# Which tiles the opening group of matmuls holds: five gate tiles in place of one branch's values and the second queries

## The chip, the cores and the metric

The kernel runs on one core of a Trainium2 chip. The metric is the device time of one execution in microseconds, the median of several runs. A profile of one execution (its page and its trace) is at hand beside the times.

## What is computed

One decoder layer on x (1 x 512 x 1024) with a condition vector c. Everything is float32. Cut to what matters here:

```python
mod = c @ w_ada + b_ada                       # six vectors of 1024: shift, scale and gate for both sub-layers
u = x * (1.0 + sc1) + sh1
proj = u @ w_in                               # q,k,v of branch A (fox), forget logits, q,k,v of branch B (stick-breaking), two gates
y_fox = softmax(q k^T/8 + c_t - c_s, causal) @ v      # 8 heads of 64, c the running sum of log sigmoid of the forget logits
y_sb  = A @ v,  A[t,s] = beta[t,s] * prod_{s<j<t} (1 - beta[t,j]),  beta = sigmoid(q k^T/8)   # 8 heads, s < t
merged = sigmoid(g_a) * (y_fox @ w_fox_proj) + sigmoid(g_b) * (y_sb @ w_sb_proj)
x = layer_norm(ALPHA * x + (1.0 + gt1) * (merged @ w_o))
h = causal_depthwise_conv((x * (1.0 + sc2) + sh2) @ w_up)
x = layer_norm(ALPHA * x + (1.0 + gt2) * ((silu(h_gate) * h_val) @ w_down))
```

## The kernel before

Every large product is made of three matmuls. An operand is split into a high part, which ACT rounds (`hi_of`, L76), and a low part, which DVE subtracts (`lo_of`, L79); high times high, high times low and low times high are summed in PSUM (L117 to L119 in `mm3`). In the code branch 1 is stick-breaking and branch 0 is fox. `PAIRS` puts the four pairs of stick-breaking heads ahead of the four fox pairs. Where a row of the profile says uh and ul, these are the two parts of u, kept for the whole attention part.

**The opening.** Eight PSUM banks `grp[0..7]` are accumulated over eight rounds j (L258 to L296), one for each 128 rows of w_in. A round loads two tiles of w_ada, 904 columns of w_in (`W1C`) and a block of x; DVE sums the condition's products (L171), ACT forms u, and PE runs 23 matmuls (L274): three for each of the banks 0 to 6 and two for bank 7. Bank 0 holds the queries of pair 0, bank 1 its keys, bank 2 the queries of pair 1, banks 3 to 6 the values of branch 1 in four blocks of tokens, bank 7 the forget logits. In the last round the banks are finished one after the other, in the order 0, 1, 2, 7, 3 to 6.

**The stream of filler.** Everything else that is projected from u is written into a list, `stream`, whose entries are generators that yield after three matmuls: `proj` (a tile of w_in of 128 columns, 24 matmuls into a new bank, then what is done with it), `vproj` (a block of values, 24 matmuls, L415 to L417), `bproj` (the projection of a branch's output, the merge), `ada_split` and `ada_sum` (the gate vector of the condition). `fill(n)` runs n matmuls of the list and `fill_to(mark)` runs up to a mark. `lim` holds a mark which `fill` doesn't pass: `y1` until head 7 has its output, then `y0`, then the end. The list's entries take weights from `items`, in order: `weights(i, ahead)` issues loads on SP's queue into four staging slots (`raw`, L133) up to item i + 3, and lets ACT and DVE process the items (split them, or sum them) up to item i + `ahead`, or earlier when a slot must be had. Among the items stand tiles of w_ada (`add_ada`, `ada_proc`): sums on DVE along the row (L171) or by column (L551). `skip` says how many of the first places for them are left out; all 24 that belong here are in the list by the end of the merge. The weights of branch 0's values are four items (`add_wv`), split into sixteen tiles of 128 x 512 (`v_proc`), and `vproj` uses them ahead of pair 4's queries.

**The attention.** The order of the heads' stages is written out at the end of the part. A head has `stage_a` (scores, L439 and L440, a mask for fox at L445, then for stick-breaking two sigmoids on ACT, a scan on DVE at L478 and a product on POOL at L479, for fox a maximum at L461, exponentials at L462 and a scaling at L467), `stage_b` (ten transposes on PE, L499, and their split) and `stage_c` (eight matmuls with the values, L517, then ytmp at L523 on ACT, yf at L524 on DVE, and on each second head yh on ACT and yl on DVE). Two heads ahead runs stage a, one ahead stage b, with fill between (`FILL`). `q_evac` and `k_evac` bring queries and keys into their parts s and m (DVE at L366 and L79); `v_evac` brings values into vv; `gate_after` takes a sigmoid of a gate's bank into sg (L580). Ahead of the first head stand the evacuations of the opening's banks with some fill between them. Most SBUF tiles of this part come from one pool of 60 (`NZ`), and PSUM is a pool of eight banks: a new tile waits for the last reader of the one that had its place.

Of the kernel before, what the change touches and what calls it, by code (L numbers as in the profile page):

```python
# [16 lines left out]
P = 128  # L17
T = 512
D = 1024
KT = D // P  # L20
NB = T // P
# [4 lines left out]
EPS = 1e-5  # L26
NEG = -1.0e30
W1C = 904
VC = slice(384, 896)
PAIRS = [(1, p) for p in range(4)] + [(0, p) for p in range(4)]  # L30
TILES = [("k", 1)]
TILES += [(c, p) for p in range(2, 8) for c in "qk"]
TILES += [("sb", j) for j in range(KT)] + [("fox", j) for j in range(KT)]
NZ = 60
LOADS = 4
WBUFS = 3
# [10 lines left out]
def layer_kernel(ctx: ExitStack, tc: tile.TileContext, out, xT, x, cT, crow, wa0, wa1, bcol, bgt, w1, wct, wv, bf,  # L47
# [74 lines left out]
    items = []  # L122
    state = {"load": 0, "proc": 0}

    def add_item(src, proc, cols=1024):
        items.append([src, proc, cols, None, None])
        return len(items) - 1

    def weights(i, ahead=AHEAD):
        while state["load"] < min(len(items), i + LOADS):  # L130
            it = items[state["load"]]
            it[3] = stg.tile([P, 1024], F32, name=nm("raw"), tag="raw", bufs=LOADS)
            nc.sync.dma_start(it[3][:, 0 : it[2]], it[0])  # L133
            state["load"] += 1
            while state["proc"] <= state["load"] - LOADS:
                process()
        while state["proc"] < min(len(items), i + 1 + ahead):
            process()
        return items[i][4]
# [19 lines left out]
    grp = [bank() for _ in range(8)]  # L159
# [98 lines left out]
    def first_ops(j, g):  # L258
        h, l = pend[j][2:4]
        a, b = uh[j], ul[j]  # L260
        if g == 7:
            return [(fpad[:, j, :], a), (fpad[:, j, :], b)]
        if g < 3:
            c = slice(g * P, (g + 1) * P)
            return [(h[:, c], a), (l[:, c], a), (h[:, c], b)]
        c = slice((g - 3) * P, (g - 2) * P)
        return [(a[:, c], h[:, VC]), (a[:, c], l[:, VC]), (b[:, c], h[:, VC])]

    def first_mm(j, gs):
        ops = [(g, n, m) for g in gs for n, m in enumerate(first_ops(j, g))]  # L270
        if j < KT - 1:
            ops.sort(key=lambda o: o[1] + 3 * (o[0] == 7))
        for g, n, (w, u) in ops:
            PE.matmul(grp[g], w, u, start=j == 0 and n == 0, stop=j == KT - 1 and n == (1 if g == 7 else 2))  # L274
# [6 lines left out]
    for j in range(KT):  # L281
        if j + 2 < KT:
            first_load(j + 2)
        if j + 1 < KT:
            with tc.issue_after(state["u"].ins):
                first_split(j + 1)
            with tc.issue_after(state["after"].ins):
                first_acc(j + 1)
        if j < KT - 1:
            first_mm(j, range(5))  # L290
        if j + 1 < KT:
            first_mod(j + 1)
        if j < KT - 1:
            first_mm(j, range(5, 8))
        else:
            first_mm(j, (0, 1, 2, 7, 3, 4, 5, 6))  # L296

    st0.close()

# [98 lines left out]
        return vt[(br, j, h // 4)][:, o : o + P]  # L398

    def v_proc(r):  # L400
        for e in range(2):
            h, l = z(F32R, "wvh"), z(F32R, "wvl")
            hi_of(h, r[:, e * 512 : (e + 1) * 512])
            lo_of(l, r[:, e * 512 : (e + 1) * 512], h)
            wvs.append((h, l))

    wvs = []

    def vproj(j, last):
        ps = bank()  # L410
        weights(last, 0)
        tb = slice(j * P, (j + 1) * P)
        for k in range(KT):
            h, l = wvs[k]
            PE.matmul(ps, uh[k][:, tb], h, start=k == 0, stop=False)  # L415
            PE.matmul(ps, uh[k][:, tb], l, start=False, stop=False)
            PE.matmul(ps, ul[k][:, tb], h, start=False, stop=k == KT - 1)  # L417
            yield 3
        for half in range(2):
            v_evac(0, j, half, ps)  # L420

    def proj(n, after):
        ps = bank()
# [198 lines left out]
    stream, sums = [], []  # L622
    adas = [0]

    skip = [15]

    def add_ada(n=1):
        for _ in range(n):
# [9 lines left out]
    marks = {}  # L638
# [17 lines left out]
    def add_pair(p):  # L656
        br, pr = seq[p]
        for c, ev in (("q", q_evac), ("k", k_evac)):
            if (c, p) in TILES:
                add_proj((c, p), lambda ps, ev=ev: ev(br, pr, ps))  # L660
                marks[(p, c)] = len(stream)
                add_ada(1 + (p > 4))
                add_wv(p)

    wvi = []

    def add_wv(p):
        if p >= 3 and len(wvi) < 4:
            wvi.append(add_item(wv[len(wvi)], v_proc))

    def add_gate(br, j):
        add_proj(("sb" if br == 1 else "fox", j), gate_after(br, j))
        add_ada(1 + (br == 0))

    gb = list(range(KT))
    for p, ng in ((1, 1), (2, 2), (3, 2), (4, 3)):
        if p == 4:
            for j in range(NB):
                stream.append((vproj, (j, wvi[-1])))
        add_pair(p)  # L680
        for _ in range(ng):
            add_gate(1, gb.pop(0))
            add_wv(p)
    marks["y1"] = len(stream)
    bj = list(range(KT))
    for p in (5, 6, 7):
        add_pair(p)
        for _ in range(3):
            if bj:
                j = bj.pop(0)  # L690
# [56 lines left out]
            fill(3)  # L747

    lim[0] = marks["y1"]
    q_evac(1, 0, grp[0])  # L750
    k_evac(1, 0, grp[1])
    forget_evac()
    q_evac(1, 1, grp[2])
    fill(6)
    stage_a(1, 0)
    for half in range(2):
        for j in range(NB):
            v_evac(1, j, half, grp[3 + j])
        fill(6)
    stage_a(1, 1)  # L760
    fill(12)
    stage_b(1, 0)
    heads = [(br, 2 * p + e) for br, p in seq for e in range(2)]
    last = hd[heads[1]]['last']
    for n, (b, h) in enumerate(heads):
        if n == 4:
            forget(last)
        f1, f2, f3 = FILL[n // 8]
        if n + 2 < 16:
            if n % 2 == 0:  # L770
                fill_to(marks[(n // 2 + 1, "k")])
            last = hd[heads[n + 1]].get("last")
            stage_a(*heads[n + 2])
        fill(f1)
        if n + 1 < 16:
            stage_b(*heads[n + 1])
        fill(f2)
        stage_c(b, h)
        if n == 7:
            lim[0] = marks["y0"]  # L780
        if n == 15:
            lim[0] = len(stream)
        fill(f3)
# [133 lines left out]
    for n in range(2 * FT):  # L917
        if n < NSPLIT:
            h, l = items[wui[n]][4]
            ps = bks[n]  # L920
# [84 lines left out]
def _pack(inputs):  # L1005
    import numpy as np

    a = {k: np.ascontiguousarray(v) for k, v in inputs.items()}
    c = np.ascontiguousarray
    w_in, w_ada = a["w_in"], a["w_ada"]  # L1010
    wk = w_ada.reshape(KT, P, 6, D)
    r = {}
    r["xT"] = c(a["x"][0].T)
    r["x"] = a["x"][0]
    r["cT"] = c(a["c"][0].reshape(KT, P).T)
    r["crow"] = a["c"]
    wt = c(w_ada.T).reshape(6, KT, P, D)
    r["wa0"] = c(wt[0:2].transpose(1, 0, 2, 3))
    kf = wk[:, :, [2, 5]].reshape(4, 2, P, 2, 2, 512).transpose(3, 4, 0, 2, 1, 5).reshape(2, 8, P, D)
    r["wa1"] = c(np.concatenate([kf[0], wt[3], wt[4], kf[1]], axis=0))  # L1020
    bm = a["b_ada"].reshape(6, KT, P)
    r["bcol"] = c(bm[[0, 1, 3, 4]].transpose(2, 0, 1))
    r["bgt"] = c(a["b_ada"].reshape(6, D)[[2, 5]])
    def col(kind, n):
        if kind in ("sb", "fox"):
            return (4104 if kind == "sb" else 3080) + n * P
        br, p = PAIRS[n]
        return 1544 * br + 512 * "qkv".index(kind) + p * P

    first = [w_in[:, s : s + P] for s in (col("q", 0), col("k", 0), col("q", 1))]  # L1030
    cols = np.concatenate(first + [w_in[:, 2568:3080], w_in[:, 1536:1544]], axis=1)
    r["w1"] = c(cols.reshape(KT, P, W1C))
    r["wv"] = c(w_in[:, 1024:1536].reshape(4, 2, P, 512).transpose(0, 2, 1, 3).reshape(4, P, D))
    starts = [col(*t) for t in TILES]
    r["wct"] = c(np.stack([w_in[:, s : s + P].reshape(KT, P, P).transpose(1, 0, 2).reshape(P, D) for s in starts]))
    r["bf"] = c(a["b_forget"].reshape(NH, 1))
    wpj = np.stack([a["w_fox_proj"], a["w_sb_proj"]]).reshape(2, 4, P, 4, 2, P)
    r["wp"] = c(wpj.transpose(0, 3, 2, 4, 1, 5).reshape(2, 4, P, D))
    r["wo"] = c(a["w_o"].reshape(KT, P, D))
    r["lncol"] = c(np.stack([a["ln1_g"].reshape(KT, P), a["ln1_b"].reshape(KT, P)]).transpose(2, 0, 1))  # L1040
    r["lnrow"] = c(np.stack([a["ln1_g"], a["ln1_b"], a["ln2_g"], a["ln2_b"]]))
    wu = a["w_up"].reshape(KT, P, 2, FT, P)
    r["wup"] = c(wu.transpose(3, 2, 1, 0, 4).reshape(2 * FT, P, D))
    cwb = np.concatenate([a["conv_w"], a["conv_b"][None]], axis=0).reshape(4, 2, FT, P)
    r["cwb"] = c(cwb.transpose(3, 2, 1, 0).reshape(P, 2 * FT, 4))
    r["wdn"] = c(a["w_down"].reshape(FT, P, D))
    return r
# [23 lines left out]
```

## Time and profile before

| What | us |
|---|---|
| Median of three runs | 769.53 |
| Lowest and highest of them | 768.99, 769.98 |
| Profiled execution | 772.13 |
| Span of its trace | 770.4 |

The span is the time between the first and the last instruction of the trace; 1.7 us of the profiled execution lie around it. The engines are PE (matmul), PEld (loading its weights), DVE, ACT, POOL, and SP, which here issues DMAs. In a row of the timeline stand the start, the duration, the engine, the line of the code, the operation, what it writes and reads, and in brackets how long the engine stood idle before it and what it then got; "x4" says that the row groups four instructions. In a row of a group the last numbers are the sum of the durations, the mean duration in ns, and the idle time ahead of the instructions. Matmuls overlap: a matmul over 512 columns lasts 0.39 us in the rows, while the next one starts after about 0.23.

### The profile page before, as it was taken

What the parts mean: (1) busy time and instruction counts of PE and PEld (TensorE: products, weight loads), DVE (VectorE), ACT (ScalarE), POOL (GpSimd) and SP (SyncE); (2) the same over time, 40 slices, a digit from 0 to 9 for tenths busy, and PEclk for the clock granted to TensorE, in tenths of its full rate; (3) what the DMA queues carried; (4) which work ended last, traced back from release to release, by engine and by line L of the source; (5) the groups of instructions that cost most, each with busy time, mean ns of one, the idle gap of its engine ahead of it and who ended that gap; (6) DMA issues with size and microseconds to landing.
All of it is one profiled execution on the core that took longest, in us unless ns stands there. A gap on an engine that the chain in (4) does not pass through costs nothing.

```text
span 770.4 us, 9543 instructions
## 1 busy us (share of the span) xinstructions
PE 752.8 (98%) x3538; PEld 622.7 (81%) x3538; DVE 548.5 (71%) x816; ACT 356.3 (46%) x590; POOL 195.1 (25%) x162
## 2 busy tenths in 40 slices
PE   7998999999999999999999999999999999999995
PEld 3876888888888887888889888888888888888885
DVE  5879879725789999685676787686656665534666
ACT  3567698526767664343145434444444433222300
POOL 1026646500010002464000770000000044945500
PEclk9999999999999999999999999999999999999999
DMA  8951133201534455553302524344322214322202
GB/s 306 405 199 63 56 111 124 69 14 70 190 124 153 162 186 191 205 191 137 137 1 80 194 83 147 118 172 137 116 102 95 97 55 165 124 94 87 105 27 83
DMA packets 31105, 99.68 MB, mean 129 GB/s; under 512 B 4273, under 2 KB 4785, under 8 KB 31058
## 3 DMA queue, kind: packets, MB, share of 16 engines
q1 hardware_dynamic: 30258, 98.72, 36.6%
q8 instruction: 28, 0.46, 0.2%
q10 hardware_dynamic: 288, 0.28, 0.2%
q14 instruction: 19, 0.16, 0.1%
q0 software_dynamic: 512, 0.07, 0.1%
HBM read 96.88 MB, written 2.10 MB: 128 GB/s over the span
## 4 chain that ended last, share of the span: by engine, by line
PE 90%; DVE 4%; ACT 2%; DMA 2%; issue 1%; SPq 0%; DVEq 0%; ACTq 0%
PE ps L117 18%; PE ps L118 18%; PE ps L119 18%; PE ps L963 5%; PE ps L964 5%; PE ps L962 5%; PE ps L274 4%; PE ps L517 2%; PE ps L499 2%; PE ps L842 2%; PE ps L843 2%; PE ps L841 2%; PE ps L439 1%; PE ps L440 1%; DVE wl L79 1%; DMA wa<-in_wa 1%
## 5 line engine op out<-in xcount | busy, mean ns | idle before, releaser
L79 DVE TENSOR_TENSOR wl<-raw,wh 128x1024 fp32r<-128x1024 f32 (+2 forms) x106 | 149.1, 1407 | 104.3 <-ACT wh L76 103.7
L76 ACT ACTIVATE wh<-raw 128x1024 fp32r<-128x1024 f32 (+2 forms) x106 | 110.2, 1041 | 105.2 <-PE ps L118 38.7
L117 PE MATMUL ps<-u2h,wh 128*128 128x512 f32 (+1 forms) x376 | 141.4, 376 | 0.0
L119 PE MATMUL ps<-u2h,wl 128*128 128x512 f32 (+1 forms) x376 | 141.2, 376 | 0.0
L118 PE MATMUL ps<-u2l,wh 128*128 128x512 f32 (+1 forms) x376 | 141.2, 376 | 0.0
L609 POOL TENSOR_TENSOR raw<-raw,gt 128x1024 f32<-128x1024 f32 x22 | 60.1, 2746 | 190.3 <-ACT cv L934 158.0
L117 PE MATMUL ps<-uh,wh 128*128 128x512 f32 x232 | 93.1, 401 | 2.7 <-DVE vv L79 2.0
L119 PE MATMUL ps<-uh,wl 128*128 128x512 f32 x232 | 91.5, 394 | 0.0
L118 PE MATMUL ps<-ul,wh 128*128 128x512 f32 x232 | 91.4, 394 | 0.0
L117 PEld LDWEIGHTS ps<-u2h,wh 128*128 128x128 f32 x376 | 70.8, 188 | 12.9
L119 PEld LDWEIGHTS ps<-u2h,wl 128*128 128x128 f32 x376 | 70.8, 188 | 12.9
L118 PEld LDWEIGHTS ps<-u2l,wh 128*128 128x128 f32 x376 | 70.8, 188 | 12.6
L117 PEld LDWEIGHTS ps<-uh,wh 128*128 128x128 f32 x232 | 44.1, 190 | 12.0 <-DVE vv L79 2.4
L119 PEld LDWEIGHTS ps<-uh,wl 128*128 128x128 f32 x232 | 44.2, 190 | 9.6
L118 PEld LDWEIGHTS ps<-ul,wh 128*128 128x128 f32 x232 | 44.1, 190 | 8.3
L963 PE MATMUL ps<-wl,hh 128*128 128x512 f32 x128 | 49.9, 390 | 0.0
L964 PE MATMUL ps<-wh,hl 128*128 128x512 f32 x128 | 49.8, 389 | 0.0
L962 PE MATMUL ps<-wh,hh 128*128 128x512 f32 x128 | 49.8, 389 | 0.0
L597 POOL TENSOR_TENSOR raw<-raw,gt 128x1024 f32<-128x1024 f32 x8 | 22.0, 2766 | 81.0 <-DVE modc L176 61.7
L76 ACT ACTIVATE hh<-cv 128x512 fp32r<-128x512 f32 x22 | 13.9, 631 | 59.7 <-DVE cv L942 59.7
L941 ACT ACTIVATE cv<-cv 128x512 f32<-128x512 f32 x22 | 13.9, 632 | 54.8 <-DVE cv L936 54.8
L479 POOL TENSOR_TENSOR pt<-pt,om 128x127 f32<-128x127 f32 (+3 forms) x32 | 34.2, 1081 | 2.7 <-DVE om L478 1.5
(192 smaller groups left out, 1476.6 us busy)
## 6 DMA issues: line engine op xcount, KB each, us to landing
raw<-in_wup SPq DMA_DIRECT2D x44, 512.0 KB, 3.2
raw<-in_wa SPq DMA_DIRECT2D x32, 512.0 KB, 3.3
raw<-in_wct SPq DMA_DIRECT2D x29, 512.0 KB, 3.4
raw<-in_wdn SPq DMA_DIRECT2D x22, 512.0 KB, 3.3
wa<-in_wa SPq DMA_DIRECT2D x14, 512.0 KB, 7.6
raw<-in_wp SPq DMA_DIRECT2D x8, 512.0 KB, 3.4
raw<-in_wo SPq DMA_DIRECT2D x8, 512.0 KB, 3.2
raw<-in_w SPq DMA_DIRECT2D x7, 452.0 KB, 7.7
```

The lines of the kernel that those rows point to most:

```text
L76: S.activation(o, i, AF.Copy, scale=scale)
L79: return V.tensor_tensor(o, i, fl(hi), ALU.subtract)
L117: PE.matmul(ps, wh, ah, start=first, stop=False)
L118: PE.matmul(ps, wh, al, start=False, stop=False)
L119: PE.matmul(ps, wl, ah, start=False, stop=last)
L274: PE.matmul(grp[g], w, u, start=j == 0 and n == 0, stop=j == KT - 1 and n == (1 if g == 7 else 2))
L479: G.tensor_tensor(pt[b][:, s : e - 1], pt[b][:, s : e - 1], om[:, s + 1 : e], ALU.mult)
L597: G.tensor_tensor(r, r, gt[0], ALU.mult)
L609: G.tensor_tensor(r, r, gt[1], ALU.mult)
L962: PE.matmul(ps, hh[j][:, tb], w[0], start=first, stop=False)
L963: PE.matmul(ps, hh[j][:, tb], w[1], start=False, stop=False)
L964: PE.matmul(ps, hl[j][:, tb], w[0], start=False, stop=last)
```

## The change

The opening keeps its eight banks and 904 columns. Banks 0 and 1 hold the queries and keys of pair 0 as before; banks 2 to 6 now hold the first five stick-breaking gate tiles; bank 7 still holds the forget logits. The last round's order is 2, 0, 1, 7, 3 to 6. What made room, the queries of pair 1 and the values of branch 1, goes into the stream: pair 1's queries and keys come first, then the four weight items of branch 1's values and four `vproj` for them, with a mark `v1` behind them, which must be reached before the first head's output. `v_proc` returns its tiles and `vproj` takes the branch; it now asks for weights two items ahead, as `proj` does. Behind the pairs 1 to 4 stand 0, 1, 1 and 1 gate tiles where there were 1, 2, 2 and 3. `skip` goes from 15 to 6, and `add_ada` puts one tile at each place, where there had been two behind the later pairs and the fox gates; each `vproj` of branch 0 has a place too. Ahead of the first head the evacuations are those of the gates, and the fill between the stages is larger.

```diff
-VC = slice(384, 896)
+NG = 5
-TILES = [("k", 1)]
-TILES += [(c, p) for p in range(2, 8) for c in "qk"]
-TILES += [("sb", j) for j in range(KT)] + [("fox", j) for j in range(KT)]
+TILES = [(c, p) for p in range(1, 8) for c in "qk"]
+TILES += [("sb", j) for j in range(NG, KT)] + [("fox", j) for j in range(KT)]
...
-        if g < 3:
-            c = slice(g * P, (g + 1) * P)
-            return [(h[:, c], a), (l[:, c], a), (h[:, c], b)]
-        c = slice((g - 3) * P, (g - 2) * P)
-        return [(a[:, c], h[:, VC]), (a[:, c], l[:, VC]), (b[:, c], h[:, VC])]
+        c = slice(g * P, (g + 1) * P)
+        return [(h[:, c], a), (l[:, c], a), (h[:, c], b)]
...
-            first_mm(j, (0, 1, 2, 7, 3, 4, 5, 6))
+            first_mm(j, (2, 0, 1, 7, 3, 4, 5, 6))
...
-    def vproj(j, last):
+    def vproj(br, j, last):
         ps = bank()
-        weights(last, 0)
+        weights(last)
         tb = slice(j * P, (j + 1) * P)
         for k in range(KT):
-            h, l = wvs[k]
+            h, l = items[wvi[br][k // 2]][4][k % 2]
...
-            v_evac(0, j, half, ps)
+            v_evac(br, j, half, ps)
...
-    skip = [15]
+    skip = [6]
...
-                add_ada(1 + (p > 4))
-                add_wv(p)
+                add_ada()
+                if p == 3:
+                    add_wv(0)
...
-        add_ada(1 + (br == 0))
+        add_ada()
-    gb = list(range(KT))
-    for p, ng in ((1, 1), (2, 2), (3, 2), (4, 3)):
+    gb = list(range(NG, KT))
+    for p, ng in ((1, 0), (2, 1), (3, 1), (4, 1)):
         if p == 4:
             for j in range(NB):
-                stream.append((vproj, (j, wvi[-1])))
+                stream.append((vproj, (0, j, len(items) - 1)))
+                add_ada()
         add_pair(p)
+        if p == 1:
+            for j in range(4):
+                add_wv(1)
+            for j in range(NB):
+                stream.append((vproj, (1, j, wvi[1][-1])))
+            marks["v1"] = len(stream)
         for _ in range(ng):
             add_gate(1, gb.pop(0))
-            add_wv(p)
+            if p in (2, 3):
+                add_wv(0)
...
     lim[0] = marks["y1"]
+    gate_after(1, 0)(grp[2])
     q_evac(1, 0, grp[0])
     k_evac(1, 0, grp[1])
     forget_evac()
-    q_evac(1, 1, grp[2])
     fill(6)
     stage_a(1, 0)
-    for half in range(2):
-        for j in range(NB):
-            v_evac(1, j, half, grp[3 + j])
-        fill(6)
+    for j in range(1, NG):
+        gate_after(1, j)(grp[2 + j])
+    fill(18)
     stage_a(1, 1)
-    fill(12)
+    fill(36)
     stage_b(1, 0)
+    fill(36)
...
         fill(f2)
+        if n == 0:
+            fill_to(marks["v1"])
         stage_c(b, h)
```

On the host the 904 columns and the tiles of the value weights of both branches are packed to match.

More of the change, by code (lines that the diff above doesn't have):

```diff
@@ L400, in v_proc @@
     def v_proc(r):
+        t = []
         for e in range(2):
@@ L404, in v_proc @@
             lo_of(l, r[:, e * 512 : (e + 1) * 512], h)
-            wvs.append((h, l))
-    wvs = []
-    def vproj(j, last):
+            t.append((h, l))
+        return t
+    def vproj(br, j, last):
         ps = bank()
-        weights(last, 0)
+        weights(last)
         tb = slice(j * P, (j + 1) * P)
         for k in range(KT):
-            h, l = wvs[k]
+            h, l = items[wvi[br][k // 2]][4][k % 2]
             PE.matmul(ps, uh[k][:, tb], h, start=k == 0, stop=False)
@@ L661, in add_pair, with add_wv @@
                 marks[(p, c)] = len(stream)
-                add_ada(1 + (p > 4))
-                add_wv(p)
[L665 to L669, printed above, removed]
+                add_ada()
+                if p == 3:
+                    add_wv(0)
+    wvi = [], []
+    def add_wv(br):
+        if len(wvi[br]) < 4:
+            wvi[br].append(add_item(wv[br, len(wvi[br])], v_proc))
     def add_gate(br, j):
         add_proj(("sb" if br == 1 else "fox", j), gate_after(br, j))
-        add_ada(1 + (br == 0))
-    gb = list(range(KT))
-    for p, ng in ((1, 1), (2, 2), (3, 2), (4, 3)):
+        add_ada()
+    gb = list(range(NG, KT))
+    for p, ng in ((1, 0), (2, 1), (3, 1), (4, 1)):
         if p == 4:
             for j in range(NB):
-                stream.append((vproj, (j, wvi[-1])))
+                stream.append((vproj, (0, j, len(items) - 1)))
+                add_ada()
         add_pair(p)
+        if p == 1:
[4 more added lines that the diff above has]
+            marks["v1"] = len(stream)
         for _ in range(ng):
             add_gate(1, gb.pop(0))
-            add_wv(p)
+            if p in (2, 3):
+                add_wv(0)
+    assert len(wvi[0]) == 4
     marks["y1"] = len(stream)
@@ L1028, in col @@
         return 1544 * br + 512 * "qkv".index(kind) + p * P
-    first = [w_in[:, s : s + P] for s in (col("q", 0), col("k", 0), col("q", 1))]
-    cols = np.concatenate(first + [w_in[:, 2568:3080], w_in[:, 1536:1544]], axis=1)
+    first = [w_in[:, s : s + P] for s in [col("q", 0), col("k", 0)] + [col("sb", j) for j in range(NG)]]
+    cols = np.concatenate(first + [w_in[:, 1536:1544]], axis=1)
     r["w1"] = c(cols.reshape(KT, P, W1C))
-    r["wv"] = c(w_in[:, 1024:1536].reshape(4, 2, P, 512).transpose(0, 2, 1, 3).reshape(4, P, D))
+    wv = np.stack([w_in[:, 1024:1536], w_in[:, 2568:3080]])
+    r["wv"] = c(wv.reshape(2, 4, 2, P, 512).transpose(0, 1, 3, 2, 4).reshape(2, 4, P, D))
     starts = [col(*t) for t in TILES]
```

## The prediction

> **What bounds the kernel now.** I read the page first, then the busy time by windows.
>
> ```profile
> span 770.4 us, 9543 instructions
> PE 752.8 (98%) x3538; PEld 622.7 (81%) x3538; DVE 548.5 (71%) x816; ACT 356.3 (46%) x590; POOL 195.1 (25%) x162
> ```
>
> ```profile
> 55.00:70.00 15.00, 12.26 (x56) 9.63 (x56) 13.81 (x22) 13.02 (x29) 11.12 (x19) 0.93 0.31 102
> 70.00:80.00 10.00, 9.67 (x48) 7.96 (x47) 9.17 (x12) 7.61 (x17) 7.75 (x9) 0.94 0.13 50
> 300.00:320.00 20.00, 18.12 (x75) 14.48 (x74) 15.39 (x21) 8.84 (x13) 7.19 (x4) 0.91 0.44 158
> 400.00:700.00 300.00, 300.00 (x1398) 251.49 (x1396) 198.15 (x227) 119.53 (x158) 76.40 (x35) 1.00 0.34 116
> ```
>
> The columns are the window, its length, busy PE, PEld, DVE, ACT and POOL, the granted clock, the DMA share and GB/s. PE works 98% of the span and all of 400 to 700. The change keeps the number of matmuls (8 rounds of 23 in the opening, and as many behind it), so it can move the time only where PE stands still or runs slowly: behind the opening (55 to 80) and around 305. The waits of PE name what came last there:
>
> ```profile
> 55.82 0.47 PE L117 MATMUL ps<-uh,wh 128*128 128x512 f32 x1 [0.76 <-DVE s L366]
> 66.61 0.50 PE L117 MATMUL ps<-uh,wh 128*128 128x512 f32 x1 [1.98 <-DVE vv L79]
> 73.86 0.39 PE L440 MATMUL ps<-m,s 68*128 68x256 f32 x1 [0.33 <-DVE m L79]
> 305.39 0.50 PE L117 MATMUL ps<-yh,wh 128*128 128x512 f32 x1 [1.88 <-ACT yh L76]
> ```
>
> The timeline of PE shows a second price behind the two long waits:
>
> ```profile
> 67.62 0.43 PE L118 MATMUL ps<-ul,wh 128*128 128x512 f32 x1
> 67.85 0.63 PE L119 MATMUL ps<-uh,wl 128*128 128x512 f32 x1
> 68.28 2.33 PE L499 MATMUL ps<-ident,pt 128*128 128x128 f32 x10
> 71.26 0.40 PE L119 MATMUL ps<-uh,wl 128*128 128x512 f32 x1
> 71.50 0.40 PE L117 MATMUL ps<-uh,wh 128*128 128x512 f32 x1
> 306.66 0.61 PE L118 MATMUL ps<-yl,wh 128*128 128x512 f32 x1
> 309.63 0.63 PE L118 MATMUL ps<-ul,wh 128*128 128x512 f32 x1
> 310.06 0.45 PE L119 MATMUL ps<-uh,wl 128*128 128x512 f32 x1
> 310.35 0.39 PE L117 MATMUL ps<-uh,wh 128*128 128x512 f32 x1
> ```
>
> Matmuls start every 0.23 us (67.62 to 67.85, 71.26 to 71.50); between 67.85 and 71.26, and again from 306.66 to 310.06, every 0.43. Each time that is 3.4 us at half rate, so 1.7 us lost. What can come back is therefore 0.76 + 1.98 + 0.33 + 1.7 = 4.8 us behind the opening and 1.88 + 1.7 = 3.6 us at 305. The start and the tail aren't touched: the opening loads the same 904 columns a round.
>
> [...]
>
> **Part 1, the opening's banks.** Removed behind it: q1's evacuation and eight value evacuations; added: five sigmoids, a projection for q1 and four value projections whose weights are split on ACT and DVE.
>
> ```profile
> L580 ACT ACTIVATE sg<-ps 128x512 f32<-128x512 f32 x16 | 9.7, 607 | 3.6 <-PE ps L119 2.8 <-POOL pt L479 0.7
> 61.48 3.30 DVE L478 TENSOR_TENSOR_SCAN om<-om,one 128x127 f32<-128x127 f32 x4
> 69.49 3.74 DVE L478 TENSOR_TENSOR_SCAN om<-om,one 128x127 f32<-128x127 f32 x4
> L366 DVE SCALAR_TENSOR_TENSOR s<-ps,s 64x512 fp32r<-64x512 f32 x16 | 11.0, 690 | 3.1 <-ACT s L76 2.7
> L79 DVE TENSOR_TENSOR m<-ps,m 64x512 fp32r<-64x512 f32 x16 | 11.0, 685 | 5.0 <-ACT m L76 4.6
> L79 DVE TENSOR_TENSOR wvl<-raw,wvh 128x512 fp32r<-128x512 f32 x8 | 7.4, 941 | 0.1
> L79 DVE TENSOR_TENSOR wol<-raw,woh 128x512 fp32r<-128x512 f32 x16 | 10.5, 684 | 0.0
> 66.96 1.94 DVE L79 TENSOR_TENSOR wl<-raw,wh 128x1024 fp32r<-128x1024 f32 x1
> 85.86 1.23 DVE L79 TENSOR_TENSOR wl<-raw,wh 128x1024 fp32r<-128x1024 f32 x1 [1.16 <-ACT wh L76]
> ```
>
> The first gate's sigmoid (0.61 on ACT, nothing on DVE) now frees the bank that q1's projection takes, so the 0.76 goes. The 1.98 was for the last value half's evacuation on DVE and goes too. DVE gets other work. In the changed order PE's way to the last pair of the first value weights is 48 projection matmuls, the 24 score matmuls of two heads, ten transposes and 36 of the value matmuls: 84 of 0.23, plus some 4.3 for scores and 1.3 for transposes, 24.8 us. DVE must by then do q0's and k0's halves (4 x 0.69), the forget sum (about 0.7), two heads' scans (3.30 + 3.74), q1's and k1's halves (4 x 0.69), one low half of transposed rows (0.5), eight value splits and three weight splits. A split costs 0.68 alone (wol) and 0.94 where POOL works beside it (wvl); a wide one 1.23 and 1.94. POOL is busy 11.12 of 15 us and 7.75 of 10 there, so I take 0.94 for the eight (7.5; bounds 5.5 and 7.5) and 3.7 to 5.8 for the three. The sum is 25.0 to 27.1. DVE got 13.81 of 15 and 9.17 of 10 us of work done in these windows, 0.92, while it waited for ACT; so 27.2 to 29.5 us pass, and PE waits 2.4 to 4.7, in pieces. I take the middle, 3.5, and 0.6 for small waits behind it: 4.1 against 4.8, **-0.7**. Bounds: with the eight splits at 0.68 and the three at 1.23, 23.0 / 0.92 = 25.0, nearly no wait, -4; with the upper sum and one half-rate window, 4.7 + 0.6 + 1.7 = 7.0, +2.2. The pieces stay below the 1.9 us that brought the clock down only if they don't fall together.
>
> The other value weights are projected later, four blocks as before, with splits among the work of heads 3 to 5:
>
> ```profile
> 110.00:160.00 50.00, 50.00 (x250) 42.37 (x249) 37.13 (x51) 33.73 (x63) 24.24 (x32) 1.00 0.25 86
> ```
>
> DVE is busy 37 of 50 us there and PE never waits; four splits of 0.94 and two more condition tiles fit into the 13 that are free; I put +0.3 there, bounds 0 and +1.
>
> **Part 2, the condition weights move ahead.** `skip` falls from 15 to 6, so nine more weight tiles of the condition go into the order before the merge's first projections, with their loads on SP's queue and sums on DVE (L171 and L551); behind it there are as many fewer. This is what undoes the wait at 305:
>
> ```profile
> 291.77 1.21 DVE L79 TENSOR_TENSOR wl<-raw,wh 128x1024 fp32r<-128x1024 f32 x1
> 295.48 1.22 DVE L171 SCALAR_TENSOR_TENSOR raw<-raw,cbc 128x1024 f32<-128x1024 f32 x1
> 296.73 0.33 SPq L133 DMA_DIRECT2D raw<-in_wct  x1
> 301.04 1.06 ACT L76 ACTIVATE wh<-raw 128x1024 fp32r<-128x1024 f32 x1 [1.79 <-DMA raw<-in_wct]
> 302.13 1.21 ACT L523 ACTIVATE ytmp<-ps 64x512 f32<-64x512 f32 x2
> 303.28 1.40 DVE L524 TENSOR_TENSOR yf<-ps,ytmp 64x512 f32<-64x512 f32 x2
> 304.71 0.63 ACT L76 ACTIVATE yh<-yf 128x512 fp32r<-128x512 f32 x1 [1.37 <-DVE yf L524]
> ```
>
> A gate's weights could be loaded only at 296.73, when the sum at 295.48 gave up its staging slot. ACT stood 1.79 us for that DMA, and ytmp, yf and yh stood in its queue behind it: the last head's output, for which PE waited. After the change that slot's predecessor is a weight split; its kin here ends at 291.77 + 1.21 = 292.98, 3.7 us before 296.7, so the DMA is there 1.9 us before ACT comes. No sum of the condition stands between yf and yh any more; what is late next is yf's own chain, which I give 0.5 us of wait, without a clock drop. **-3.1**, bounds -3.6 (nothing left) and 0 (another transfer in its place).
>
> **Part 3, filler in the last stick-breaking heads.** The gate tiles among the filler are fewer, and `fill` may not run past the mark `y1`, so heads 6 and 7 of the first branch lack 41 matmuls (9.3 us) between their stages. PE then meets q5's projection early. It needs the bank of head 6's output, which yf frees.
>
> ```profile
> 179.64 1.69 DVE L461 TENSOR_REDUCE sm<-ps 128x1 f32<-128x128 f32 x4
> 182.58 1.28 DVE L467 TENSOR_SCALAR pt<-pt,sm 128x128 f32<-128x128 f32 x4
> L171 DVE SCALAR_TENSOR_TENSOR raw<-raw,cbc 128x1024 f32<-128x1024 f32 x16 | 19.3, 1212 | 0.2
> L524 DVE TENSOR_TENSOR yf<-ps,ytmp 64x512 f32<-64x512 f32 x16 | 11.0, 687 | 4.4 <-ACT ytmp L523 4.2
> ```
>
> Let T be the end of the first fox head's scores. On PE follow 13 matmuls, two sums, two outputs, a score stage and 20 transposes: 3.0 + 0.5 + 2.5 + 1.7 + 2.5, so PE stands at that projection at T + 10.2. On DVE follow from T + 0.6: four reduces (1.69), one condition sum (1.21), one row of the gate vector (0.7), the four scalings (1.28), three low halves (1.7), three reduces (1.2), a weight split (1.23) and yf (0.69), 9.7 in all, and 1.25 of waiting for ACT's exponentials as between 181.33 and 182.58: T + 11.6. PE waits some 1.5 us: **+1.5**. Bounds: 0, if the split stands elsewhere (its 1.23 gone), and +3.5 with a half-rate window (1.5 + 0.3 + 1.7). A wait behind DVE holds the later q5 and k5 only; the fox heads behind them have filler again.
>
> **Sum.** -0.7 + 0.3 - 3.1 + 1.5 = -2.0 us: a span of 768.4, a profiled time of 770.1 where it was 772.13 (1.7 around the span), and against the median of the runs, which lies 2.6 below the profiled one, 769.53 - 2.0 = **767.5 us**.
>
> **The rivals.**
> *The gains are eaten up (no change).* The wait at 305 stays behind another load (0 for -3.1: +1.1, 770.6); or the new wait at q5 drops the clock (+3.5 for +1.5: 0, 769.5); or the half-rate stretch at 306.66 has another cause than the wait ahead of it and stays, so that only 1.88 - 0.5 = 1.4 come back there (-0.3, 769.2). For it: these shifts are as large as the whole forecast. Against the last: both slow stretches begin within 1.3 us of the only two waits of 1.9 us behind the start. [...]
> *DVE behind the opening becomes the bound (slower).* All four value weights must be split before PE can finish the first value block, in the very stretch in which DVE is busy 92%. If the handoffs to ACT cost twice the idle time (0.84 instead of 0.92), 27.1 / 0.84 = 32.3 us pass; PE waits 7.5, and with 0.6 and one half-rate window 9.8 us, 5.0 more than before. Then 5.0 + 0.3 - 3.1 + 1.5 = +3.7, 773.2. It decides from the point at which PE loses over 7.6 us there, since the other terms sum to -1.3 (7.6 - 4.8 - 1.3 = +1.5). For it speaks DVE's 9.17 of 10; against it, that the eight value evacuations that stood ahead of the second head's scans move behind the splits.
> *More gain.* DVE's splits run at their price alone and q5's wait is hidden: -4 - 3.1 + 1.5 to 0, about -5.2: 764.3.
>
> **How the numbers follow.** A difference of 0.2%, 1.5 us, is about what a measurement of this kernel can tell. The forecast with the greater gain behind it (over 1.5 faster) has 0.42, the first rival 0.30, the second 0.28. The range goes from 764.3 to 772.6, short of the far end of the second rival; the forecast's own case is 764.3 to 768.0.
>
> **What would show it.** Right: no wait over 0.5 us near 305 and no half-rate stretch behind it; in its place a wait of about 1.5 us for DVE's yf at q5's projection, some 15 to 20 us behind the first fox scores; the 0.76 gone; several waits of 0.3 to 1.2 for wvl in 60 to 85, in sum about 4. Wrong: a second half-rate stretch in 60 to 90, a wait for DMA ahead of the first value weights, or the wait at 305 in front of another load. A span change that lies outside 55 to 320 would refute the whole reading.

## The result, and the profile after

| Kernel | Median, us | Ratio to before | 95% interval |
|---|---|---|---|
| before | 769.4 | 1 | |
| changed | 780.75 | 1.0138 | 1.0123 to 1.0154 |

The median before has here a fourth execution beside the three of the table above. The change makes the kernel 1.4% slower, 11.4 us by the medians, where the prediction had 2.0 us faster. The profiled execution took 780.92 us, its span 779.2. Line numbers have moved, by one to eight: L116 to L118 are the three matmuls that were L117 to L119, L170 and L547 the condition's sums (L171, L551), L435 and L436 scores, L495 transposes, L513 the products with the values, L411 to L413 `vproj`, L520 yf.

The page's first lines of the changed kernel:

```profile
span 779.2 us, 9558 instructions
PE 756.1 (97%) x3538; PEld 622.2 (80%) x3538; DVE 550.4 (71%) x820; ACT 353.4 (45%) x591; POOL 197.4 (25%) x162
```

The other engines' busy times are nearly the same. The span grew by 8.8 us: PE stands 23.1 us where it stood 17.6, and its own busy time is 3.3 us longer, for the same number of matmuls. The busy time by windows (columns as in the prediction) says where; the last row is 160 to 180 in the kernel before:

```profile
55.00:70.00 15.00, 14.59 (x68) 11.51 (x67) 12.13 (x16) 13.11 (x28) 12.78 (x16) 1.00 0.19 72
70.00:80.00 10.00, 8.87 (x43) 6.65 (x42) 8.05 (x11) 7.56 (x13) 4.11 (x6) 1.00 0.36 131
160.00:180.00 20.00, 13.17 (x46) 9.88 (x45) 17.50 (x29) 9.01 (x18) 4.47 (x7) 0.74 0.67 236
300.00:320.00 20.00, 20.00 (x99) 16.73 (x98) 12.96 (x17) 8.43 (x14) 4.86 (x3) 1.00 0.39 131
...
160.00:180.00 20.00, 19.82 (x92) 16.07 (x92) 6.64 (x11) 8.51 (x13) 0.62 (x2) 1.00 0.15 53
```

Behind the opening PE now stands 1.5 us in 25 and the clock is 1.00 (it was 3.1 us, at 0.93 and 0.94); 300 to 320 is full (it lost 1.9, at 0.91). Both places got better. The loss lies in 160 to 180: 6.8 us idle, and a granted clock of 0.74, where before PE stood 0.2 us and the clock was 1.00. The waits of PE in the changed kernel, by what came last, with their sum, their number and the longest:

```profile
PE ps L495 <- DVE yf L520: 4.6, 1, 4.6
PE ps L163 <- DMA cbr<-in_crow: 2.3, 1, 2.3
PE ps L411 <- DVE vv L78: 2.1, 1, 2.1
PE ps L850 <- DVE wol L78: 1.1, 2, 0.8
PE ps L412 <- DVE wvl L78: 1.0, 1, 1.0
PE ps L270 <- ACT uh L236: 0.9, 2, 0.6
PE ps L116 <- DVE yf L520: 0.8, 1, 0.8
```

The first and the third are the new ones: transposes of a head that want the bank which an earlier head frees with yf, and a value block that wants a bank which vv frees. Between and behind them PE runs at half rate, as its timeline shows (0.43 us between matmuls until 179.5, 0.23 from 181):

```profile
169.89 0.90 PE L495 MATMUL ps<-ident,pt 128*128 128x128 f32 x3 [4.64 <-DVE yf L520]
174.22 0.80 PE L411 MATMUL ps<-wvh,uh 128*128 128x512 f32 x1 [2.15 <-DVE vv L78]
178.65 0.63 PE L412 MATMUL ps<-wvl,uh 128*128 128x512 f32 x1
179.08 0.63 PE L413 MATMUL ps<-wvh,ul 128*128 128x512 f32 x1
181.17 0.40 PE L412 MATMUL ps<-wvl,uh 128*128 128x512 f32 x1
181.40 0.39 PE L413 MATMUL ps<-wvh,ul 128*128 128x512 f32 x1
```

What kept yf is in the timelines of ACT, DVE and SP's queue in the same stretch:

```profile
164.22 0.59 ACT L519 ACTIVATE ytmp<-ps 64x512 f32<-64x512 f32 x1
...
163.63 0.48 DVE L542 TENSOR_SCALAR ac<-raw,cTs 128x512 f32<-128x512 f32 x1
164.57 4.68 DVE L547 SCALAR_TENSOR_TENSOR ac<-raw,cTs,ac 128x512 f32<-128x512 f32 x6
169.16 0.68 DVE L520 TENSOR_TENSOR yf<-ps,ytmp 64x512 f32<-64x512 f32 x1
171.13 1.23 DVE L78 TENSOR_TENSOR wl<-raw,wh 128x1024 fp32r<-128x1024 f32 x1 [0.63 <-ACT wh L75]
172.27 0.42 DVE L78 TENSOR_TENSOR vv<-ps,vv 128x256 fp32r<-128x256 f32 x1
172.60 1.22 DVE L170 SCALAR_TENSOR_TENSOR raw<-raw,cbc 128x1024 f32<-128x1024 f32 x1
...
165.34 0.33 SPq L132 DMA_DIRECT2D raw<-in_wct  x1
...
170.03 1.06 ACT L75 ACTIVATE wh<-raw 128x1024 fp32r<-128x1024 f32 x1 [5.22 <-DMA raw<-in_wct]
```

Six sums for the second half of the first gate vector stand in one row on DVE, 4.68 us, ahead of the yf that PE waits for; the operand of yf was there at 164.8 (ytmp on ACT starts at 164.22 and takes 0.59). The same sums hold the staging slots: the load of the next projection's weights (`in_wct`) is issued at 165.34, when the first of the six is through, ACT waits 5.22 us for it, and the value halves vv stand behind it in ACT's and DVE's queues. That is the second wait. PE starts the next `proj` only at 183.68, so these weights were not urgent; what stood behind them was.

The slots had been full for some time. Three of the condition tiles were loaded from 135.83, 140.60 and 147.50 on and left their slots only from 165.3 on; between 152.77 and 162.94 SP issued no load at all, and the DMA engines and DVE were far from busy:

```profile
155.00:160.00 5.00, 4.89 (x25) 3.96 (x23) 2.27 (x3) 2.34 (x5) 3.15 (x5) 1.00 0.04 16
```

The trace doesn't show why the first of these sums stands on DVE only at 163.63.

A mark that is the same in both kernels is the first matmul of each head's output. Head by head, less the work that stands in another order (0.228 us a matmul), the changed kernel is 4.3 us ahead at head 0 (1.4 of it from the opening's end, see the last section), 3.9 at head 3, then 8.9 behind at head 5: 12.8 lost. The two waits are 6.8 of this and the half-rate stretches about 3.5; the rest is in pieces from 148 on, the largest a wait of 0.60 for sg at 150.59. It is 10.7 behind at head 8, 7.0 behind the place of the old wait at 305, and 9.0 behind at the end of the output projection, where it waits 0.84 and 0.23 us for wol. The small wait at q5 stands between head 5 and head 8:

```profile
210.76 0.50 PE L116 MATMUL ps<-uh,wh 128*128 128x512 f32 x1 [0.77 <-DVE yf L520]
```

### The profile page after: what moved, and what is told of

Read it like the earlier page. It is cut to its first block, busy times and chain, and to the rows that moved or that the text cites. A ratio compares the mean times of both kernels' runs of the same rounds, so it can differ in the third digit from the quotient of the medians.

```text
span 779.2 us, 9558 instructions
## 1 busy us (share of the span) xinstructions
PE 756.1 (97%) x3538; PEld 622.2 (80%) x3538; DVE 550.4 (71%) x820; ACT 353.4 (45%) x591; POOL 197.4 (25%) x162
## 4 chain that ended last, share of the span: by engine, by line
PE 73%; DVE 9%; ACT 7%; issue 4%; DMA 4%; POOL 3%; SPq 0%; DVEq 0%; ACTq 0%; POOLq 0%
PE ps L116 14%; PE ps L117 14%; PE ps L118 14%; PE ps L970 5%; PE ps L971 5%; PE ps L972 5%; PE ps L270 4%; DVE wl L78 3%; ACT wh L75 2%; ACT m L75 1%; PE ps L513 1%; PE ps L495 1%; PE ps L850 1%; PE ps L851 1%; PE ps L849 1%
## 5 line engine op out<-in xcount | busy, mean ns | idle before, releaser
L78 DVE TENSOR_TENSOR wl<-raw,wh 128x1024 fp32r<-128x1024 f32 (+2 forms) x102 | 147.2, 1444 | 91.6 <-ACT wh L75 91.0
L75 ACT ACTIVATE wh<-raw 128x1024 fp32r<-128x1024 f32 (+2 forms) x102 | 106.0, 1040 | 93.2 <-PE ps L972 38.3
L116 PE MATMUL ps<-u2h,wh 128*128 128x512 f32 (+1 forms) x376 | 141.5, 376 | 0.0
L118 PE MATMUL ps<-u2h,wl 128*128 128x512 f32 (+1 forms) x376 | 141.4, 376 | 0.0
L117 PE MATMUL ps<-u2l,wh 128*128 128x512 f32 (+1 forms) x376 | 141.4, 376 | 0.0
L118 PEld LDWEIGHTS ps<-u2h,wl 128*128 128x128 f32 x376 | 70.8, 188 | 12.9
L117 PEld LDWEIGHTS ps<-u2l,wh 128*128 128x128 f32 x376 | 70.8, 188 | 12.8
L116 PEld LDWEIGHTS ps<-u2h,wh 128*128 128x128 f32 x376 | 70.8, 188 | 12.7
L116 PE MATMUL ps<-uh,wh 128*128 128x512 f32 x200 | 79.3, 397 | 0.8 <-DVE yf L520 0.8
L118 PE MATMUL ps<-uh,wl 128*128 128x512 f32 x200 | 78.2, 391 | 0.0
L117 PE MATMUL ps<-ul,wh 128*128 128x512 f32 x200 | 78.2, 391 | 0.0
L116 PEld LDWEIGHTS ps<-uh,wh 128*128 128x128 f32 x200 | 37.6, 188 | 8.2 <-DVE yf L520 1.0
L118 PEld LDWEIGHTS ps<-uh,wl 128*128 128x128 f32 x200 | 37.6, 188 | 8.0
L117 PEld LDWEIGHTS ps<-ul,wh 128*128 128x128 f32 x200 | 37.7, 188 | 7.0
```

Source lines behind the costliest of these rows:

```text
L75: S.activation(o, i, AF.Copy, scale=scale)
L78: return V.tensor_tensor(o, i, fl(hi), ALU.subtract)
L116: PE.matmul(ps, wh, ah, start=first, stop=False)
L117: PE.matmul(ps, wh, al, start=False, stop=False)
L118: PE.matmul(ps, wl, ah, start=False, stop=last)
```

## The experiments

Two theories were set against each other. A: the condition tiles that now stand at the value projections of branch 0 stop PE. B: splitting that branch's value weights in heads 4 and 5, with banks and SBUF tiles full, is enough. Later C: not DVE's time, but that a condition tile holds one of the four staging slots.

**Undo the condition part.**

```diff
-    skip = [6]
+    skip = [11]
...
-                add_ada()
+                add_ada(1 + (p > 4))
...
-        add_ada()
+        add_ada(1 + (br == 0))
...
                 stream.append((vproj, (0, j, len(items) - 1)))
-                add_ada()
```

> The changed kernel with the condition's weight tiles as before: none ahead of the merge's first projections (skip 11), two per place behind it, none at the value projections. Theory A (the burst of condition sums between the value projections of branch 0 stops PE around 165 to 178): that stall goes, the gain behind the opening stays (about 4.3 us by the trace), the wait at 305 comes back (3.6): 765 to 769 us. Rival B (splitting the value weights in heads 4 and 5, with banks and pool slots full, is enough to stop PE): 775 us or more.

Measured: 767.33 us, ratio 0.998 (0.997 to 0.9989). Its waits of PE:

```profile
PE ps L163 <- DMA cbr<-in_crow: 2.2, 1, 2.2
PE ps L116 <- ACT yh L75: 2.1, 1, 2.1
PE ps L412 <- DVE wvl L78: 1.0, 1, 1.0
PE ps L435 <- ACT m L75: 0.8, 3, 0.5
```

No wait near 165 is left, and 160 to 180 is full; the wait at 305 is back. The value weights alone do not stop PE: B falls, and the whole of the loss, some 13 us, comes with the condition tiles.

**The condition part alone, on the kernel before.**

```diff
-    skip = [15]
+    skip = [6]
...
-                add_ada(1 + (p > 4))
+                add_ada()
...
-        add_ada(1 + (br == 0))
+        add_ada()
...
-                stream.append((vproj, (j, wvi[-1])))
+                stream.append((vproj, (j, len(items) - 1)))
+                add_ada()
```

> The kernel before with the condition's tiles spread as in the change (skip 6, one per place, one at each of the four value projections), the opening as before. Theory A: a stall at the value projections appears here too, 5 to 11 us, the wait at 305 goes: 771 to 777 us. Rival B: no new stall, only the gain at 305: 765 to 767 us.

Measured: 778.7 us, 1.0124 (1.0109 to 1.0139), a little above what A said. PE has two new great waits, both ahead of scores: 3.66 us at 128.65 among the value weights and 4.77 at 184.77 ahead of the first fox scores. The list of waits by causes:

```profile
PE ps L439 <- ACT m L76: 4.9, 2, 4.8
PE ps L440 <- DVE m L79: 4.0, 2, 3.7
```

Ahead of both ACT waited for weights (`in_wct`): 3.96 us at 118.51, and 7.8 in three waits between 130 and 200. With the old opening the stages fall on other places of the stream, and the keys' evacuation (m) is held up instead of yf. The condition part costs 9.5 us without the new opening, by the medians, and 13.4 with it.

**Only the four tiles at the value projections.**

```diff
-                add_ada()
+                add_ada(1 + (p > 4))
                 if p == 3:
...
                 stream.append((vproj, (0, j, len(items) - 1)))
-                add_ada()
```

> The changed kernel without the four condition tiles at the value projections of branch 0 (they move behind the merge's start, where the queries and keys get two per place). Theory A: the stall around 165 to 178 goes almost wholly: 766 to 771 us. Rival B: 777 us or more. If it is the condition's sums anywhere ahead of the merge, about half of the loss stays: 774.

Measured: 771.11 us, 1.0023 (1.0009 to 1.0037): at the far end of A's range. The four tiles make some 9.6 of the loss; the five that stay ahead of the merge, among the value weights, still cost PE two waits for m:

```profile
144.75 0.39 PE L436 MATMUL ps<-m,s 68*128 68x256 f32 x1 [1.01 <-DVE m L78]
148.20 0.60 PE L435 MATMUL ps<-m,s 128*128 128x512 f32 x1 [2.48 <-DVE m L78]
```

**DVE's time or the slots?** The sums leave out all but 16 columns.

```diff
-            acc = ada_st[g]
+            acc = ada_st[g][:, 0:16] if n < 8 else ada_st[g]
...
-                    V.scalar_tensor_tensor(acc, r[:, e * 512 : (e + 1) * 512], cTs...
+                    V.scalar_tensor_tensor(acc, r[:, e * 512 : e * 512 + (16 if n < 8 else 512)], cTs...
```

> The changed kernel whose sums for the first gate vector take 16 columns instead of 512 for all but the first product (the gate vector is not fully summed); all loads and their order stay. Theory A with DVE's time as the cause: DVE is free for yf and the value halves, the stall of 4.6 us goes: 768 to 773 us. Rival C (the staging slots and the late loads of weights are the cause, ACT's 5.2 us wait for its DMA): 777 us or more.

Measured: 778.93 us, 1.0126 (1.0104 to 1.0147). Most of DVE's time in the bunch is gone, and PE waits as long (3.8 for yf and 3.0 for vv). The timelines of DVE, SP and ACT of this kernel:

```profile
160.67 1.85 DVE L547 SCALAR_TENSOR_TENSOR ac<-raw,cTs,ac 128x16 f32<-128x16 f32 x7
165.28 1.22 DVE L78 TENSOR_TENSOR wl<-raw,wh 128x1024 fp32r<-128x1024 f32 x1 [2.76 <-ACT wh L75]
166.43 0.67 DVE L520 TENSOR_TENSOR yf<-ps,ytmp 64x512 f32<-64x512 f32 x1
...
160.92 0.33 SPq L132 DMA_DIRECT2D raw<-in_wct  x1
...
164.20 1.06 ACT L75 ACTIVATE wh<-raw 128x1024 fp32r<-128x1024 f32 x1 [3.90 <-DMA raw<-in_wct]
165.28 0.59 ACT L519 ACTIVATE ytmp<-ps 64x512 f32<-64x512 f32 x1
```

The bunch takes 1.85 us, but the weights' load is still issued only when its first sums free a slot (160.92); ACT waits 3.90 for it, and ytmp, and so yf, stand behind that wait. In the changed kernel ytmp stood ahead of the weights on ACT (164.22 and 170.03), so this edit moved the order of the queue too. The run shows that the loss stays without most of the sums' time, held by the late load instead. That speaks for C, but it doesn't part DVE's time cleanly from the slots.

**A fifth slot.** The room for it comes from one SBUF tile and one constant (`zerob`) fewer.

```diff
-NZ = 60
-LOADS = 4
+NZ = 59
+LOADS = 5
...
```

> The changed kernel with five staging slots instead of four (room made by one SBUF tile fewer in the pool, 59 for 60, and one constant less). If the loss is that a condition tile holds one of four slots until its sum comes up, so that the load of the next weights is issued too late: the waits of ACT for its DMA and of PE at 165 to 178 shrink by more than half, 769 to 775 us. If it is the order of work on DVE and ACT alone: 779 us or more.

Measured: 785.29 us, 1.0203 (1.019 to 1.0217), slower still. C as it was put falls: more slots alone don't mend it. DVE's timeline (L519, L541, L546 and L169 are here the lines L520, L542, L547 and L170):

```profile
168.35 1.22 DVE L169 SCALAR_TENSOR_TENSOR raw<-raw,cbc 128x1024 f32<-128x1024 f32 x1 [1.81 <-DMA raw<-in_wa]
169.50 0.48 DVE L541 TENSOR_SCALAR ac<-raw,cTs 128x512 f32<-128x512 f32 x1
170.02 3.90 DVE L546 SCALAR_TENSOR_TENSOR ac<-raw,cTs,ac 128x512 f32<-128x512 f32 x5
173.84 0.68 DVE L519 TENSOR_TENSOR yf<-ps,ytmp 64x512 f32<-64x512 f32 x1
```

Now a sum along the row (L169) that waits for its own tile stands ahead of the bunch, and yf still behind all of it. With one slot more the loads run one item further ahead, and the next weights after 157.1 are again loaded only at 169.6, behind the condition tiles.

**The control for it**, 59 SBUF tiles with four slots and the same constant fewer.

> The control for five slots: the changed kernel with 59 SBUF tiles in the pool, four slots as before. If the lost tile made five slots slower: 785 us. If it was the fifth slot itself: 781.

Measured: 777.69 us, 1.0093 (1.0077 to 1.0109). So the missing tile doesn't cost; the fifth slot does, 7.6 us. Why it costs that much is not settled: the trace with five slots has the wait at yf (5.2), waits of 0.4 to 1.8 us ahead of scores in five places, and 1.7 us more behind the opening. The control itself is 3 us faster than the changed kernel, which neither case foresaw: its trace has no wait of PE for yf near 165, but 2.31 and 1.04 us for m at 145 and 147 and 2.20 for ptc at 171. So even one tile fewer moves the loss to other places in the same stretch, and single waits should not be taken for the cause.

**Small tiles.** The first twelve tiles with 64 columns in load and sum, so the sums leave out the others; the lines below are the load's side.

```diff
...
-                add_item(wa1[adas[0]], ada_proc(adas[0]))
+                few = 64 if adas[0] < 12 else 1024
+                add_item(wa1[adas[0]][:, 0:few], ada_proc(adas[0]), few)
...
```

> The changed kernel with the first twelve condition tiles loaded and summed over 64 columns instead of 1024 (the gate vector and four shifts are then wrong); order, slots and waits stay. If the bytes of the bunched loads make the weights late: the waits for DMA at the value projections go, 768 to 772 us. If it is the order in which slots come free and the fixed time of a load: 775 us or more.

Measured: 778.19 us, 1.0109 (1.0092 to 1.0125). Neither the bytes nor the sums' time alone: ACT still waits 3.9 us for `in_wct`, whose load is issued at 161.95 when the bunch starts to free its slots, ytmp stands behind it as in the run with short sums, and PE waits 3.8 for yf. Only the second wait (vv) shrinks, to 0.2.

**Don't ask ahead.** In the change each value projection of branch 0 asks for weights up to the item that stands just ahead of it in the list and two items more, among them condition tiles. Here it asks for its own four alone; the list is the same.

```diff
-        weights(last)
+        weights(last, AHEAD if br else 0)
...
-                stream.append((vproj, (0, j, len(items) - 1)))
+                stream.append((vproj, (0, j, wvi[0][-1])))
```

> The changed kernel with the same list of items, but the value projections of branch 0 ask only for their own four weight items and none ahead (before, the change lets each ask for the tile behind it and two more). If the sums and splits that each value projection puts into the queues of DVE and ACT ahead of the running head's output are the cause: 768 to 774 us. If the tiles in the list cost the time wherever they are asked for: 779 us or more, since the next query projection then asks for all of them at once.

Measured: 775.73 us, 1.0067 (1.0054 to 1.008): between the two. DVE's and SP's timelines tell both halves:

```profile
163.94 0.68 DVE L520 TENSOR_TENSOR yf<-ps,ytmp 64x512 f32<-64x512 f32 x1 [0.19 <-ACT ytmp L519]
...
177.61 4.68 DVE L547 SCALAR_TENSOR_TENSOR ac<-raw,cTs,ac 128x512 f32<-128x512 f32 x6
182.32 0.68 DVE L362 SCALAR_TENSOR_TENSOR s<-ps,s 64x512 fp32r<-64x512 f32 x1
...
178.38 0.33 SPq L132 DMA_DIRECT2D raw<-in_wct  x1
```

yf now runs as its operand comes (DVE stands 0.19 us for it), the wait of 4.6 is 0.33, and the clock is 1.00 in 160 to 180. But the bunch only moves to where the next queries ask for everything at once: six sums ahead of s, the weights' load at 178.38, and waits of PE of 1.56, 1.01 and 0.96 us at 186 to 200. So the loss depends on where in the queues the bunch stands, and what it holds up moves with it.

**Five slots without early tiles**, on the first experiment's kernel.

> The first experiment's kernel (no condition tile ahead of the merge) with five staging slots. The wait at 305 there has the same cause, a load issued late because a condition sum holds the slot: with a fifth slot it goes with its half-rate stretch, 763 to 765 us. If that wait is not one of slots: 767.

Measured: 774.34 us, 1.0066 (1.0051 to 1.0081). The wait at 305 stays (2.8 us), so the number of slots alone isn't its cause either. The kernel is 7.0 us slower than the first experiment's; the fifth slot seems to cost here too, though no control with 59 tiles was run on this kernel.

**Thin out the tiles around 305.** On the first experiment's kernel, one condition tile instead of two behind the fox gates 2, 3, 6 and 7.

```diff
-        add_ada(1 + (br == 0))
+        add_ada((1 + (j not in (2, 3, 6, 7))) if br == 0 else 1)
```

> The first experiment's kernel with one condition tile instead of two behind the fox gates 2, 3, 6 and 7, so that fewer sums stand on DVE around the last heads. If the wait at 305 is a condition sum ahead of yf on DVE and in the slots: it goes, 764 to 766 us. If not: 767.

Measured: 765.66 us, 0.9936 (0.9923 to 0.9949): faster than both kernels. The wait is gone; ACT's wait for the weights ahead of the last outputs too, since their load is out at 288.46:

```profile
288.46 0.33 SPq L132 DMA_DIRECT2D raw<-in_wct  x1
...
294.81 1.06 ACT L75 ACTIVATE wh<-raw 128x1024 fp32r<-128x1024 f32 x1 [1.19 <-issue]
296.38 0.60 ACT L519 ACTIVATE ytmp<-ps 64x512 f32<-64x512 f32 x1
...
297.74 1.40 DVE L520 TENSOR_TENSOR yf<-ps,ytmp 64x512 f32<-64x512 f32 x2
```

**The same number, thinned later** (two behind gates 0 to 3, one behind 4 to 7).

> As the one before, but two tiles behind the fox gates 0 to 3 and one behind 4 to 7, so that the place just ahead of the wait at 305 keeps its two. Same cause: the wait stays, 767 us.

Measured: 768.64 us, 0.9975 (0.9965 to 0.9984). The wait stays (2.44 us), as expected. It is the place of the tiles, not their number.

**The thinning on the kernel before.**

> The kernel before with the same thinning of condition tiles behind the fox gates 2, 3, 6 and 7 and nothing else of the change. It tells what the new opening is worth beside it. If the opening gains what the waits of the traces say (about 3.3 us of wait and half-rate stretch, less the wait of 0.5 that it adds at the fox scores): this stays 2 to 3 us above the kernel thinned with the new opening, so 0.996 to 0.997 of the time before. If the opening is worth nothing: 0.9936, as that one.

Measured: 768.25 us, 0.9976 (0.9965 to 0.9986). The wait at 305 is 1.15 instead of 1.88. Against 0.9936 with the new opening: the opening by itself is worth some 0.4%, 3.1 us, a little more than expected, and is not what made the kernel slower.

## Why the prediction was wrong, point by point

- **Part 1, behind the opening: right in kind, too small.** The 0.76 and the 1.98 went, and several waits for wvh and wvl came: 0.34, 0.96 and 0.16, in sum 1.5 us where 4.1 was forecast, and no half-rate stretch (the clock is 1.00 in 55 to 80). By these waits the gain is 3.3 us (forecast 0.7), and thinned kernels with the old and the new opening differ by 3.1. The three weight splits took 1.22 to 1.23 us each, the lower price and not the middle, and the eight value splits some 6.0 in all where 7.5 was taken. The price of 0.94 "where POOL works beside it" was misread: it is the mean of splits of 0.68 to 1.28, and of two with POOL busy all through them one took 0.69 (at 128.0) and one 1.28 (at 136.1). The eight splits still end at 81.0, 27.7 us behind the opening's end, as computed; but PE has more than the 24.8 us of work ahead of the last pair, since matmuls of the second value block run between those of the first.
- **Part 1, the value weights of branch 0, and part 2, the tiles that move ahead: the step that failed.** "+0.3, bounds 0 and +1" was read from DVE's free time over 50 us (37 of 50 busy; "four splits of 0.94 and two more condition tiles fit into the 13 that are free"); the other seven of the nine tiles that move ahead of the merge were priced at nothing. The marks of the heads give 12.8 us there. DVE's sum of time did fit: DVE was busy 40.0 of 50 us in 110 to 160 and 17.5 of 20 in 160 to 180. What the sum doesn't show is that the sums come in a bunch of six, that a head's yf stands behind them in DVE's queue though its operand is there, that the next weights' load waits for the slots which they hold, and that two PE waits of 4.6 and 2.1 us are followed by half rate (some 7 us of work at 0.43 instead of 0.23, 3.5 lost). That the tiles cost the time is shown: taking them away takes away the whole loss, with the old opening they cost too, and asking for them later moves the loss. How much of it is DVE's time and how much the slots is not parted: taking away DVE's time or the bytes takes little, but both edits also changed the order on ACT.
- **Part 2, the wait at 305: right.** It went with its half-rate stretch: 10.6 us behind ahead of it, 7.0 after it, so -3.6 (forecast -3.1). The thinning shows the cause that was given, condition tiles ahead of the last heads' outputs, though a fifth slot didn't mend it, so it is their place, on DVE and in the order of loads, rather than the number of slots; which of the two was not tested.
- **Part 2, the end of the list: missed.** The last condition tile now stands between the last weights of the merge and the last three of the output projection, and PE waits 0.84 and 0.23 us for wol; by the marks some 2 us. The order of the last loads was not followed to its end, and this loss lies outside the stretch of 55 to 320 to which the prediction confined the change. That this tile is the reason was not tested: the third experiment's kernel, which has none there, has no such wait, but the thinned one, which has none either, waits 0.9 us.
- **Part 3, the gap at q5: right.** 0.77 us for yf at 210.76, as named, and 0.43 for m at 223.96; by the marks 1.8 from head 5 to head 8 (forecast 1.5).
- **The rivals.** The one on the slower side named the right kind of mechanism, splits on DVE that PE must wait for, in the wrong place: the opening, where the time fell. Its sign was right, its price (+3.7) a third, so the right direction was luck. The case with more gain is added up wrongly: -4 + 0.3 - 3.1 and nothing at q5 is -6.8, not -5.2; the measured time lies far on the other side.

The terms as measured: -2.5 behind the opening, +12.8, +1.8, -3.6 and +2.0 make +10.5; the spans from the opening's end differ by 10.2 (725.9 against 715.7), and the medians by 11.4.

What stays open: why a fifth staging slot costs 7 us, with the early tiles and without; what keeps the bunch back until 163.63; and it wasn't tried to put yf ahead of the sums on DVE while the tiles stay, which would price the queue's order by itself.

## What to carry to other kernels

Free time of an engine over a stretch doesn't price work that is moved into it: look at which instruction will stand right behind it in that engine's queue, and who waits for that one. Work that "has time" is better spread one piece at a time, and kept out of the stretches in which the same loads and slots bring the weights that PE needs next; the thinning at 305 bears this out, at 165 it was not tried. A change of several parts can hold a gain: here the opening was worth 0.4%, while the tiles moved beside it lost 1.6%; a thinning that was no part of the change brought 0.2 to 0.4%.

## What the runs showed of the hardware that was not expected

- The same wait does not always cost the same. Before, PE's waits of 1.98 and 1.88 us were each followed by 3.4 us at half rate, and so was the wait of 2.79 us at 305 with five slots and no early tiles (0.43 us between matmuls from 306.91 to 310.28). The wait of 2.10 us at 302 in the first experiment and that of 2.44 at 303 in the later-thinned kernel were not: behind both the matmuls start every 0.23 us, and the clock is 1.00 in 300 to 320 and in 300 to 330. So the 1.7 us that the prediction adds to a wait of 1.9 is no fixed price, and the length of a wait alone doesn't say whether it falls due; no run here shows what does.
- The opening's last matmul starts at 54.67 us in the profiled execution before and at 51.96 in the second experiment, which has the same opening; over all the profiles it lies between 51.96 and 54.67. So profiled spans are compared here from the opening's end.
